# Values of the second layer projected with tokens on the partitions, and the bonus as one column per token

## The chip, the cores and the metric

The kernel runs on one core of one Trainium2 chip. The metric is the device time of one execution in microseconds. Before the change it is 4623.11 us, the median of 3 runs (4621.35 to 4625.97).

## The reference

One inference step of a two-layer streaming encoder. It works on a prompt of 2048 tokens and on 8 running streams of 16 tokens each, with 1024 channels, all in fp32. The first layer is a gated DeltaNet mixer, the second an RWKV-7 time mixer; each adds its output to x, and a last RMS norm follows. The change lies in the second layer alone:

```python
rkvz = jnp.einsum('gbtd,dge->gbte', xs[:4], w_in.reshape(D, 4, W_B)).astype(f32)
r, k, v, z = rkvz[0], rkvz[1], rkvz[2], rkvz[3]
...
k = k * (1.0 + (a - 1.0) * k_a.astype(f32))
...
S, o = lax.scan(step, s0.astype(f32), seq)
...
o = (o - mean) * lax.rsqrt(var + GN_EPS) * gn_w + gn_b
o = o + jnp.sum(r * k * r_k.astype(f32), axis=-1, keepdims=True) * v
o = o.reshape(B, T, W_B) * jax.nn.silu(z)
y = o.astype(h.dtype) @ w_out
```

There are 16 heads of 64 channels. The values v enter twice: in the recurrence over tokens (the scan), and in the bonus, the sum over a head's channels of r, k and r_k, times v. The bonus's sum is one number per token and head.

## The kernel before, in words

Every projection is done with split operands: each fp32 matrix is a high and a low part in fp32r, and three products (high by high, high by low, low by high) make one. On TensorE the stationary operand is the one that is loaded first, the moving one streams past it, and the result has as many rows as the stationary one has columns.

The second layer works on 6 blocks of tokens (`B_BLOCKS`): the first has 2 chunks of 64 prompt tokens and the 128 sample tokens (256 columns), the five others 6 chunks each (384 columns). Its work is of two kinds.

*The stream* (`b_stream`) projects the blocks: for each block the kinds k (1), r (0), the two low-rank hidden layers (4, 5), v (2) and z (3), in units of 128 output channels, two units at a time, each in a PSUM bank of its own (tag "mm", 2 banks). A pair of units is 8 steps; a step takes one weight tile of 128x256 and makes 6 products (lines 1062 to 1064). The weight tile is stationary and the tokens move, so the result has channels on the partitions and tokens in the columns. `b_keep` copies a finished bank on ScalarE (line 1084) and stores it to DRAM (`kvd`). Where v is needed, its tile is loaded again as V (line 1097), again with channels on the partitions. The stream runs about one block ahead of the rest.

*The pair steps* (`b_steps`) work on 48 pairs (8 pairs of heads in 6 blocks). In step i five stages of different pairs run beside each other: `b_prep` of pair i, `b_subst` of i-1, `b_inverse` of i-2, `b_scan` of i-3, `b_gate` of i-4, and `b_out` of two finished pairs at each second step, and 17 steps of the stream (8 in the last 8 pairs). A step has 12 rounds (`rounds`). A stage written as a generator gets its next piece in the round given for it, in the order prep, inverse, gate, subst, scan, out, stream. This order holds on TensorE alone, which is the one engine in `MANUAL`.

On the other engines and on the DMA queue of SyncE a list scheduler orders the instructions by due times. `_due` computes these from the log of all instructions: an instruction's due time is the place of the first TensorE instruction that needs what it writes, less a lead (6 places, 40 for a DMA), through as many instructions as lie between; what nobody needs soon gets a slack of 300 places.

Where the values and the bonus come in before the change:

- `b_prep` forms kp (line 1159) and rk = r times r_k times kp (line 1163) on VectorE. In round 5 TensorE makes the sums of squares of the keys as one column per chunk (line 1188). In round 7 the bonus's sum is one product with a block matrix of 0.5 (line 1198), which gives the sum on every channel row, and VectorE multiplies it with V (line 1200): `bv`.
- `b_inverse` turns V, chunk by chunk and head by head, with the identity (line 106, from `turn`) in its fifth piece, which is round 5, and ScalarE copies the result into `XV` (line 1327), which the scan reads.
- `b_scan` has for each chunk a product with XV (line 1382), a second product (1393) and the state's update by VectorE into the next chunk's part of XV (line 1395) and into R (line 1396).
- `b_centre` and `b_gate` normalise the scan's output OC with tokens on the partitions (line 1476 on GpSimd is the last pass), turn it back in round 6 (line 106), then on VectorE multiply with the norm's weight, add bv (line 1485), add the norm's bias and multiply with the z path (line 1486). The result is split (lines 162 and 163) for `b_out` (lines 168 to 170).

## Time and profile before

| | |
|---|---|
| profiled execution | 4610.68 us |
| its span, first to last instruction | 4608.9 us |
| TensorE busy | 4299.8 us (93%) |
| VectorE busy | 3470.3 us (75%) |
| ScalarE busy | 2287.8 us (50%) |
| GpSimd busy | 1749.9 us (38%) |
| mean granted TensorE clock | 0.966 |

One execution is profiled, and its durations are those of the rows below. PE is TensorE, PEld its weight loads, DVE VectorE, ACT ScalarE, POOL GpSimd, SP SyncE. L1198 is line 1198 of the kernel. An fp32 product shows as two instructions, an fp32r product as one. Products are pipelined: their ends are modelled and overlap, so the distance of two starts tells what one takes of the engine's time.

### The profile page before, as it was taken

What the parts mean: (1) busy time and instruction counts of PE and PEld (TensorE: products, weight loads), DVE (VectorE), ACT (ScalarE), POOL (GpSimd) and SP (SyncE); (2) the same over time, 40 slices, a digit from 0 to 9 for tenths busy, and PEclk for the clock granted to TensorE, in tenths of its full rate; (3) what the DMA queues carried; (4) which work ended last, traced back from release to release, by engine and by line L of the source; (5) the groups of instructions that cost most, each with busy time, mean ns of one, the idle gap of its engine ahead of it and who ended that gap; (6) DMA issues with size and microseconds to landing.
All of it is one profiled execution on the core that took longest, in us unless ns stands there. A gap on an engine that the chain in (4) does not pass through costs nothing. (4 is left out here: it accounts for less than half of the span.)

```text
span 4608.9 us, 104071 instructions
## 1 busy us (share of the span) xinstructions
PE 4299.8 (93%) x37093; PEld 3697.1 (80%) x37093; DVE 3470.3 (75%) x9203; ACT 2287.8 (50%) x6132; POOL 1749.9 (38%) x2507
## 2 busy tenths in 40 slices
PE   7999999999999999999987889999999999999996
PEld 6888788888888899999986767778787887887775
DVE  7888776676666776766677888877778778777885
ACT  5554454454344434444466665655455446446543
POOL 7666543322111211112103555445444434344441
PEclk9999999999999999999998989999999999999997
DMA  6666665556445576666655667766675665665542
GB/s 192 210 202 207 211 208 172 174 187 192 142 140 159 174 212 186 183 213 188 179 159 175 206 196 229 223 179 196 191 203 166 197 206 163 201 195 146 145 129 72
DMA packets 765670, 842.18 MB, mean 183 GB/s; under 512 B 263480, under 2 KB 497360, under 8 KB 765152
## 3 DMA queue, kind: packets, MB, share of 16 engines
q1 hardware_dynamic: 765152, 835.53, 59.9%
q8 instruction: 294, 4.82, 0.4%
q14 instruction: 224, 1.84, 0.1%
HBM read 632.73 MB, written 202.53 MB: 181 GB/s over the span
## 5 line engine op out<-in xcount | busy, mean ns | idle before, releaser
L453 PE MATMUL ps<-hh,whl 128*128 128x384 f32 (+1 forms) x1960 | 795.3, 406 | 12.8 <-ACT hh L162 10.6
L455 PE MATMUL ps<-hh,whl 128*128 128x384 f32 (+1 forms) x1960 | 711.8, 363 | 6.9 <-POOL whl L125 6.7
L454 PE MATMUL ps<-hl,whl 128*128 128x384 f32 (+1 forms) x1960 | 710.9, 363 | 1.7 <-DVE hl L163 1.4
L1062 PE MATMUL ps<-xh,whl 128*128 128x384 f32 (+1 forms) x1632 | 605.3, 371 | 32.0 <-ACT xh L162 17.4
L1063 PE MATMUL ps<-xl,whl 128*128 128x384 f32 (+1 forms) x1632 | 557.8, 342 | 22.0 <-POOL xl L163 11.2
L1064 PE MATMUL ps<-xh,whl 128*128 128x384 f32 (+1 forms) x1632 | 556.8, 341 | 9.2 <-DVE whl L125 8.8
L125 POOL TENSOR_TENSOR whl<-wraw,whl 128x256 fp32r<-128x256 f32 x454 | 374.6, 830 | 358.6 <-ACT whl L124 331.5
L573 DVE SCALAR_TENSOR_TENSOR cv<-pre,cw,cv 128x512 f32<-128x512 f32 (+3 forms) x576 | 375.3, 660 | 134.9 <-ACT cv L571 130.2
L453 PEld LDWEIGHTS ps<-hh,whl 128*128 128x128 f32 x1960 | 371.9, 190 | 65.8 <-issue 14.1
L168 PE MATMUL ps<-oh,whl 128*128 128x384 f32 (+2 forms) x1024 | 390.3, 381 | 26.6 <-DMA whl<-wd 13.9
L124 ACT CAST whl<-wraw 128x256 fp32r<-128x256 f32 x726 | 287.2, 402 | 255.5 <-DMA wraw<-in_w_b 74.3
L455 PEld LDWEIGHTS ps<-hh,whl 128*128 128x128 f32 x1960 | 371.4, 189 | 48.2 <-POOL whl L125 12.7
L454 PEld LDWEIGHTS ps<-hl,whl 128*128 128x128 f32 x1960 | 372.7, 190 | 34.0 <-DVE hl L163 4.6
L1062 PEld LDWEIGHTS ps<-xh,whl 128*128 128x128 f32 x1632 | 320.7, 197 | 75.3 <-ACT xh L162 23.0
L169 PE MATMUL ps<-ol,whl 128*128 128x384 f32 (+2 forms) x1024 | 366.8, 358 | 7.6 <-DVE ol L163 7.6
L844 DVE TENSOR_TENSOR sbt<-B,TB 48x15 f32<-48x15 f32 (+14 forms) x1320 | 351.9, 267 | 22.3 <-DMA B<-scr 1.7
L170 PE MATMUL ps<-oh,whl 128*128 128x384 f32 (+2 forms) x1024 | 363.6, 355 | 1.8 <-POOL whl L125 1.8
L846 DVE TENSOR_TENSOR TB<-TB,sbt 48x15 f32<-48x15 f32 (+14 forms) x1320 | 348.9, 264 | 19.8
L1063 PEld LDWEIGHTS ps<-xl,whl 128*128 128x128 f32 x1632 | 322.5, 198 | 33.8 <-POOL xl L163 17.2
L1064 PEld LDWEIGHTS ps<-xh,whl 128*128 128x128 f32 x1632 | 321.7, 197 | 16.8 <-DVE whl L125 16.2
L822 DVE TENSOR_TENSOR x<-x,ps 128x384 f32<-128x384 f32 (+1 forms) x320 | 191.1, 597 | 79.4 <-PE ps L170 77.9
L168 PEld LDWEIGHTS ps<-oh,whl 128*128 128x128 f32 x1024 | 196.6, 192 | 66.1 <-ACT oh L162 10.7
(349 smaller groups left out, 10233.7 us busy)
## 6 DMA issues: line engine op xcount, KB each, us to landing
whl<-wd SPq DMA_DIRECT2D x1582, 256.0 KB
wd<-whl SPq DMA_DIRECT2D x428, 256.0 KB
wraw<-in_w_a SPq DMA_DIRECT2D x288, 128.0 KB
wraw<-in_w_b SPq DMA_DIRECT2D x256, 128.0 KB
kvd<-kvo SPq DMA_DIRECT2D x160, 192.0 KB
xn<-x1d SPq DMA_DIRECT2D x80, 192.0 KB
wraw<-in_w_ao SPq DMA_DIRECT2D x96, 128.0 KB
xn<-in_x SPq DMA_DIRECT2D x32, 256.0 KB
```

What stands on the lines that cost most here:

```text
L125: (self.nc.gpsimd if tag == "o" else self.weng).tensor_tensor(w[:, 1], raw, w[:, 0].bitcast(F32), op=SUB)
L168: self.nc.tensor.matmul(out, lhsT=wh, rhs=hh, start=first and i == 0, stop=False)
L169: self.nc.tensor.matmul(out, lhsT=wh, rhs=hl, start=False, stop=False)
L170: self.nc.tensor.matmul(out, lhsT=wl, rhs=hh, start=False, stop=i == n - 1)
L453: nc.tensor.matmul(p, lhsT=wh[:, k % 2], rhs=hh, start=k == 0, stop=False)
L454: nc.tensor.matmul(p, lhsT=wh[:, k % 2], rhs=hl, start=False, stop=False)
L455: nc.tensor.matmul(p, lhsT=wl[:, k % 2], rhs=hh, start=False, stop=k == KT - 1)
L573: nc.vector.scalar_tensor_tensor(o, f(j), self.cw[:, ct, j:j + 1], o, op0=MUL, op1=ADD)
L844: nc.vector.tensor_tensor(o, B[:, j + 1:16, j:j + 1].to_broadcast([rows, m, j + 1]), T[:, j:j + 1, 0:j + 1].to_broadcast([rows, m, j + 1]) ...
L1062: nc.tensor.matmul(o, lhsT=wh[:, i], rhs=xh, start=k == 0, stop=False)
L1063: nc.tensor.matmul(o, lhsT=wh[:, i], rhs=xl, start=False, stop=False)
L1064: nc.tensor.matmul(o, lhsT=wl[:, i], rhs=xh, start=False, stop=k == KT - 1)
```

## The change

In the stream the values' units are computed the other way round: the token tile `xh[:, ts]` of 128 tokens is stationary, and 256 columns of the weights move, two units at once. The weight tile of a step now holds one of the 8 input tiles for 256 output channels (two pieces of 512 bytes a row in the first load). The result has tokens on the partitions. Of the 384 tokens two tiles of 128 share the first bank and the third lies in the second; since three sums begin in two banks, a product of a zero tile with 512 columns clears the first bank. `b_keep_values` copies each token tile on ScalarE and stores it to `vt` in DRAM, tokens as rows. V is no longer loaded and not turned: `b_inverse` loads each head's values from `vt` straight into XV.

The bonus's sum becomes one column per chunk in `b_prep`, as the keys' sums are, right behind them in round 5; ScalarE halves it (`bs`). The bonus times the values is formed by GpSimd in `b_inverse` with tokens on the partitions, and is added in `b_gate` before the turn back. So the norm's weight is multiplied there too, by a table `gw` whose rows repeat over the tokens; behind the turn one VectorE pass is left.

```diff
-NCI, NXH, NOH, NKO = 2, 8, 2, 2
+NCI, NXH, NOH, NKO = 2, 8, 2, 3
...
+                    if g == 2:
+                        self.b_values(b, 2 * s + j, wh, wl, p)
+                        if s == 3 and j:
+                            self.b_keep_values(b, first[1], p)
...
+    def b_values(self, b, k, wh, wl, p):
+
+        xh, xl = b["X", 2, k]
+        wh, wl = [w.rearrange("p j c -> p (j c)") for w in (wh, wl)]
+        if k == 0:
+            self.nc.tensor.matmul(p[0], lhsT=self.zero.to_broadcast([P, P]), rhs=wh.unsqueeze(1).to_broadcast([P, 2, 256]), start=True, stop=False)
+        for t in range(b["NT"] // P):
+            o, ts = p[t // 2][:, t % 2 * 256:t % 2 * 256 + 256], slice(t * P, (t + 1) * P)
+            self.nc.tensor.matmul(o, lhsT=xh[:, ts], rhs=wh, start=k == 0 and t == 2, stop=False)
+            self.nc.tensor.matmul(o, lhsT=xl[:, ts], rhs=wh, start=False, stop=False)
+            self.nc.tensor.matmul(o, lhsT=xh[:, ts], rhs=wl, start=False, stop=k == KT - 1 and t > 0)
+
+    def b_keep_values(self, b, q, p):
+        for t in range(b["NT"] // P):
+            v = self.sp.tile([P, 256], F32, name=self.nm("kvo"), tag="kvo", bufs=NKO)
+            self.nc.scalar.copy(v, p[t // 2][:, t % 2 * 256:t % 2 * 256 + 256])
+            self.nc.sync.dma_start(b["vt"][t * P:(t + 1) * P, q * P:q * P + 256], v)
...
-        for g, n, bufs in ((1, "K", 2), (0, "R", 1), (2, "V", 3)):
+        for g, n, bufs in ((1, "K", 2), (0, "R", 1)):
...
+        pb = self.ps("g")
+        for c in range(nq):
+            for h, hs in enumerate(HS):
+                nc.tensor.matmul(pb[HS[1 - h], c:c + 1], lhsT=c3(rk)[hs, c], rhs=self.ones[hs, 0:1], start=True, stop=True,
+                                 tile_position=(64 * h, 64 - 64 * h))
...
-        pbn = self.ps("g")
-        nc.tensor.matmul(pbn[:, 0:NT], lhsT=cb[:, B_BO:B_BO + P], rhs=rk, start=True, stop=True)
-        bv = self.lp.tile([P, NT], F32, name=self.nm("bv"), tag="bv", bufs=4)
-        nc.vector.tensor_tensor(bv, pbn[:, 0:NT], V, op=MUL)
+        bs = self.mp.tile([P, 8], F32, name=self.nm("bs"), tag="bs", bufs=3)
+        nc.scalar.activation(bs[:, 0:nq], pb[:, 0:nq], AF.Copy, scale=0.5)
...
+        for h in range(2):
+            os, vs = HS[1 - h], slice(q * P + 64 * h, q * P + 64 * h + 64)
+            nc.sync.dma_start(XV[os, 0:nq, h], vt[:, :, vs])
...
-        pt = self.ps("g")
-        for c in range(nq):
-            for h, hs in enumerate(HS):
-                self.turn(pt[HS[1 - h], c * 64:(c + 1) * 64], c3(V)[hs, c], h, 1 - h)
...
-            nc.scalar.copy(XV[os, 0:nq, h], c3(pt[os, 0:nq * 64]))
+            nc.gpsimd.tensor_tensor(bv[os], XV[os, 0:nq, h], d["bs"][os, 0:nq].unsqueeze(2).to_broadcast([64, nq, 64]), op=MUL)
...
+        nc.vector.tensor_tensor(OC, OC, self.gw[:, q:q + 1].to_broadcast([P, nq, 64]), op=MUL)
+        nc.vector.tensor_tensor(OC, OC, d["bv"], op=ADD)
...
-        og = d["bv"]
-        nc.vector.scalar_tensor_tensor(og, pu[:, 0:NT], self.hp[:, q, 3:4], og, op0=MUL, op1=ADD)
-        nc.vector.scalar_tensor_tensor(og, og, self.hp[:, q, 4:5], SZ, op0=ADD, op1=MUL)
+        og = d["bv"].rearrange("p c v -> p (c v)")
+        nc.vector.scalar_tensor_tensor(og, pu[:, 0:NT], self.hp[:, q, 4:5], SZ, op0=ADD, op1=MUL)
```

## Rows read from the trace of the kernel before

**Rows 1.** Windows, one pair step: us, engines' busy us (count), clock, DMA share, GB/s.

```profile
3363.60:3415.50 51.90, 48.06 (x531) 41.82 (x530) 37.47 (x93) 20.68 (x58) 22.97 (x27) 0.93 0.71 205
```

**Rows 2.** Waits of TensorE, 2800 to 4400 us: us in total, times, longest.

```profile
PE ps L1382 <- DVE XV L1395: 37.5, 28, 2.6
```

**Rows 3.** Groups of instructions by shape: count | busy us, mean ns | idle before.

```profile
L106 PE MATMUL ps<-ident,V 64*64 64x64 f32 x1088 | 43.0, 225 | 0.0
...
L1188 PE MATMUL ps<-ones,ch 64*64 64x1 f32 x1088 | 40.3, 196 | 4.1 <-POOL ch L1161 4.1
...
L1198 PE MATMUL ps<-ch,cb 128*128 128x384 f32 x80 | 33.8, 504 | 2.3 <-DVE ch L1163 1.9 <-DVE TB L846 0.4
```

**Rows 4.** Timeline of TensorE, behind the bonus: start us, us, instruction, idle before it.

```profile
2911.03 0.81 PE L1198 MATMUL ps<-ch,cb 128*128 128x384 f32 x2
2911.77 0.34 PE L1382 MATMUL ps<-XV,GM 128*64 128x64 f32 x4
...
3373.57 0.80 PE L1382 MATMUL ps<-XV,GM 128*64 128x64 f32 x4 [2.25 <-DVE XV L1395]
```

**Rows 5.** Timeline of VectorE, the scan's state at the same two places.

```profile
2909.99 0.59 DVE L1395 SCALAR_TENSOR_TENSOR XV<-ps,wc,Sw 64x64 f32<-64x64 f32 x2
...
3372.72 0.60 DVE L1485 SCALAR_TENSOR_TENSOR bv<-ps,hp,bv 128x384 f32<-128x384 f32 x1
3373.25 0.59 DVE L1395 SCALAR_TENSOR_TENSOR XV<-ps,wc,Sw 64x64 f32<-64x64 f32 x2
3373.88 0.62 DVE L1486 SCALAR_TENSOR_TENSOR bv<-bv,hp,SZ 128x384 f32<-128x384 f32 x1
```

**Rows 6.** Timeline of TensorE, products of 256 and of 384 columns.

```profile
2508.38 0.28 PE L1064 MATMUL ps<-xh,whl 128*128 128x256 f32 x1
...
2508.73 0.28 PE L1064 MATMUL ps<-xh,whl 128*128 128x256 f32 x1
...
3302.17 0.34 PE L169 MATMUL ps<-ol,whl 128*128 128x384 f32 x1
...
3303.05 0.34 PE L1062 MATMUL ps<-xh,whl 128*128 128x384 f32 x1
```

**Rows 7.** Timelines of TensorE and ScalarE, between two pairs of the values' units.

```profile
2468.24 0.38 PE L1062 MATMUL ps<-xh,whl 128*128 128x256 f32 x1
...
2467.82 0.37 ACT L1084 COPY kvo<-ps 128x256 f32<-128x256 f32 x1
...
3131.62 0.44 PE L1062 MATMUL ps<-xh,whl 128*128 128x384 f32 x1
...
3131.23 0.48 ACT L1084 COPY kvo<-ps 128x384 f32<-128x384 f32 x1
```

**Rows 8.** Timelines of VectorE and TensorE: kp, rk and the keys' column products.

```profile
3451.47 0.54 DVE L1159 TENSOR_TENSOR ch<-ch,K 128x384 f32<-128x384 f32 x1
...
3459.12 0.60 DVE L1163 SCALAR_TENSOR_TENSOR ch<-R,prm,ch 128x384 f32<-128x384 f32 x1
...
3453.16 0.69 PE L1188 MATMUL ps<-ones,ch 64*64 64x1 f32 x18
```

**Rows 9.** Timelines of GpSimd and TensorE: the gate's last pass and its turn.

```profile
3363.44 0.83 POOL L1476 TENSOR_TENSOR OC<-OC,gn 128x384 f32<-128x384 f32 x1
...
3368.03 0.92 PE L106 MATMUL ps<-ident,OC 64*64 64x64 f32 x24
```

**Rows 10.** Lines 1225 and 1236 (ns min/median/max), then timelines of GpSimd and VectorE.

```profile
L1225 POOL TENSOR_TENSOR N<-GM,m x36: 827/1020/1137, 2837.8 to 4395.4; 64x384 f32<-64x384 f32 x36
...
L1236 SPq DMA_DIRECT2D scrb<-N x72: 577/581/1375, 2843.5 to 4397.4; - x72
...
3462.10 4.48 POOL L1181 TENSOR_TENSOR BK<-ch,ch 64x384 f32<-64x384 f32 x4 [0.51 <-ACT ch L1152]
...
3462.23 1.03 DVE L846 TENSOR_TENSOR TB<-TB,sbt 48x39 f32<-48x39 f32 x1
...
3366.81 0.18 DVE L846 TENSOR_TENSOR TB<-TB,sbt 48x39 f32<-48x39 f32 x1
```

More of the change, by code (lines that the diff above doesn't have):

```diff
@@ L908, in b_setup_side @@
         nc.vector.tensor_scalar(mu[:, 1], mu[:, 0], -1.0, 1.0, op0=MUL, op1=ADD)
+        self.zero = bp.tile([P, 1], F32R, name="zero")
+        nc.gpsimd.memset(self.zero.bitcast(F32), 0.0)
         hc = bp.tile([P, KT, 1], F32, name="hc")
@@ L922, in b_setup @@
         nc.vector.tensor_scalar(hp[:, :, 5:6], hp[:, :, 2:3], -1.0, 1.0, op0=MUL, op1=ADD)
+        gw = bp.tile([P, KT, 64], F32, name="gw")
+        for h in range(2):
+            nc.sync.dma_start(gw[64 - 64 * h:P - 64 * h].rearrange("p q v -> p (q v)"), io["b_gw"][h, :].partition_broadcast(64))
+        nc.vector.tensor_scalar(gw, gw, 0.5, None, op0=MUL)
+        self.gw = gw
         sm = bp.tile([P, NB], F32, name="smb")
@@ L1039, in srcs @@
                     for j in range(2):
-                        yield ("b", g, q, s, j), w[:, s, 2 * j:2 * j + 2], b["off"]
+                        yield ("b", g, q, s, j), w[:, s, j:4:2] if g == 2 else w[:, s, 2 * j:2 * j + 2], b["off"]
         yield from self.b_hidden(blocks[0])
@@ L1057, in b_stream @@
                     wh, wl = next(W)
+                    if g == 2:
+                        self.b_values(b, 2 * s + j, wh, wl, p)
+                        if s == 3 and j:
+                            self.b_keep_values(b, first[1], p)
                     o = p[j][:, 0:NT]
-                    for i in range(2):
+                    for i in range(2 if g != 2 else 0):
                         k = 2 * s + i
@@ L1064, in b_stream @@
                         nc.tensor.matmul(o, lhsT=wl[:, i], rhs=xh, start=False, stop=k == KT - 1)
-                    if s == 3:
+                    if s == 3 and g != 2:
                         self.b_keep(b, g, q, p[j])
@@ L1271, in b_inverse @@
         T, Tt = Ts
+        ex = 2 * b["nsc"]
+        TM = self.lp.tile([P, nq + ex, 2, 64], F32, name=self.nm("TM"), tag="TM", bufs=2)
+        XV = self.lp.tile([P, nq + ex, 2, 64], F32, name=self.nm("XV"), tag="XV", bufs=2)
+        VS = self.lp.tile([P, 2 * ex, 64], F32, name=self.nm("VS"), tag="VS", bufs=2) if ex else None
+        assert (2, q) in b["kept"]
+        vt = b["vt"].rearrange("(c t) x -> t c x", t=64)
+        for h in range(2):
+            os, vs = HS[1 - h], slice(q * P + 64 * h, q * P + 64 * h + 64)
+            nc.sync.dma_start(XV[os, 0:nq, h], vt[:, :, vs])
+            if ex:
+                nc.sync.dma_start(VS[os, 0:ex], vt[:, ncp:nq, vs])
         N16 = self.lp.tile([P, ncp, 64], F32, name=self.nm("N16"), tag="ci", bufs=NCI)
@@ L1318, in b_inverse @@
         yield
-        pt = self.ps("g")
-        for c in range(nq):
-            for h, hs in enumerate(HS):
-                self.turn(pt[HS[1 - h], c * 64:(c + 1) * 64], c3(V)[hs, c], h, 1 - h)
-        if ex:
-            nc.scalar.copy(VS[:, 0:ex], c3(pt[:, ncp * 64:nq * 64]))
+        bv = self.lp.tile([P, nq, 64], F32, name=self.nm("bv"), tag="bv", bufs=3)
         for h in range(2):
             os = HS[1 - h]
-            nc.scalar.copy(XV[os, 0:nq, h], c3(pt[os, 0:nq * 64]))
+            nc.gpsimd.tensor_tensor(bv[os], XV[os, 0:nq, h], d["bs"][os, 0:nq].unsqueeze(2).to_broadcast([64, nq, 64]), op=MUL)
+        d["bv"] = bv
         yield
```

14 lines of the change are left out of this document (7 added, 7 removed).

## The prediction

> **What bounds the kernel now.** I read the page's busy times first, then the windows of single pair steps, then the waits of TensorE, and then the timelines of TensorE and VectorE where the diff cuts. The second layer runs from about 2450 us to the end, 48 pair steps of 25 to 57 us. In an ordinary step TensorE is busy 48.06 of 51.90 us, VectorE 37.47, ScalarE 20.68, GpSimd 22.97, and the granted clock there is 0.93 [rows 1]. So TensorE's work sets the pace, and what it doesn't work is short waits. The largest of these is for one thing: in the 1600 us from 2800 to 4400 the scan product on line 1382 waited 37.5 us, 28 times, for the state that VectorE writes on line 1395 [rows 2]. A microsecond taken off TensorE's queue is therefore a microsecond won only where no such wait stands right behind it. Where one does, VectorE's order decides. I price each part with this test.
>
> **The change part by part.**
>
> *The bonus product goes.* Line 1198 is one fp32 product of 384 columns per pair, shown as two instructions, 504 ns each [rows 3]. From its start to the next start on TensorE it holds the queue 0.74 us (2911.03 to 2911.77) [rows 4]. What comes right behind it is, from the twelfth pair on, the scan product of line 1382, and I went through all 48 places in the timeline. In 14 of them the state had been written long before, as here, where VectorE was done at 2910.58 [rows 5], 1.19 us before the scan product: these win all of 0.74, together 10.4 us. In 12 TensorE stands idle behind the bonus until line 1395 is done, as at 3373.57 after 2.25 us [rows 4]: these win nothing. In 11 the state came within that 0.74 us: they win 3.0 us together. In the first 11 pairs a projection or output product follows, and the starts are 0.24 to 0.6 us apart: 3.7 us. Sum: 17.1 us off the path, of some 33 us of queue. Bounds: 0 and 33.
>
> *The turn of the values goes, the bonus column comes.* In round 5 of a step stand today 24 instructions that turn the values (line 106) behind 24 one-column products (line 1188). After the change 24 more one-column products stand in the place of the turn. 1088 turns took 43.0 us and 1088 one-column products 40.3 us [rows 3]: I take nothing, bound 2.7 us of gain. ScalarE loses two copies of the turned values and gains one tiny scaling. It is off the path, and I take nothing for that.
>
> *The bonus column needs its input two rounds earlier.* The products of round 5 now read rk (line 1163), which the old bonus product read in round 7. In 30 of the 48 pairs rk was finished only after round 5's products had started. The typical case: products at 3453.16, rk done at 3459.72, while kp, its input on line 1159, was done at 3452.01 [rows 8]. Taken over all pairs the lateness adds up to 113 us. But rk was not late for lack of input: it lay ready some 7 us and VectorE did other things, because the planner's due time came from round 7. With the new due time it can run right behind kp, and be done 0.6 us after it [rows 8], before the product. Kp itself ended after the products in nine pairs, all among the first twelve and the last three, by some 31 us in all when rk's 0.6 is counted behind it; kp's due time moves with rk's, and I leave an eighth: +4 us. Bounds: 0 and +113. Behind the waiting column stand, in TensorE's one queue, the scan step of that round and a projection.
>
> *The values' projection.* Six old products of 384 columns per chunk become nine of 256. Starts are 0.176 us apart at 384 columns (five steps from 3302.17 to 3303.05) and 0.117 us at 256 (three steps from 2508.38 to 2508.73) [rows 6], and there too each product has its own weight load. 72 times 0.117 is 8.4 us, 48 times 0.176 is 8.4 us: nothing. The clearing product of 512 columns is new, 24 times; by twice the 256 pitch it is 0.235 us: +5.7 us.
>
> *Both banks come full together.* Before, the bank of the first unit was copied out while the second was still being filled. Now the next pair of units waits for two ScalarE copies of 256 columns, 0.37 us each [rows 7]. In the later blocks the next projection starts at 3131.62 where ScalarE began its copy at 3131.23: two copies end at 3131.97, 0.35 us late. Such a busy ScalarE stands at some 8 of the 20 boundaries: 2.8 us. In the first block the next product follows at 2468.24 and two copies from 2467.82 end at 2468.56 [rows 7], and at another of the four ScalarE came a microsecond later: 0.7 us each, 2.8 us. Together +5.6 us, bounds 0 and 18 (24 times 0.74).
>
> *The gate.* VectorE gains two passes over OC ahead of the turn back and loses the product on line 1200 and one of the two passes behind the turn, lines 1485 and 1486: an equal number. Ahead of the turn there is room: OC was ready at 3364.27 and turned at 3368.03 [rows 9], one of the closest of the ordinary steps; most have 7 to 18 us. Only the last pair of all has none: two passes more before and one less behind is one pass of 0.6 us at the end of the kernel, +0.6. The pass that goes behind the turn matters more. In nearly all pairs from the ninth on, line 1485 stands right ahead of line 1395 in VectorE's order: 3372.72, then the state at 3373.25, then line 1486 at 3373.88 [rows 5]. If the one remaining pass takes line 1486's place, the state is 0.53 us earlier: 12 idle places give 6.4 us and the 11 half-covered ones 4.5 us more. If it takes line 1485's place, nothing comes. I take -8. Bounds: -11 and 0.
>
> *GpSimd and the loads.* The bonus times the values is two products of 64x384 with a broadcast on GpSimd; the nearest row is line 1225, 1.02 us [rows 10]. Two microseconds of an engine that idles half of each step [rows 1], needed only two steps later: hidden, but they may push another GpSimd product: +2, bounds 0 and 26 (below). The load of V (one issue) becomes two loads into XV of 64 rows and 256-byte pieces, issued in round 1 of the third step and used from round 5. The nearest row on SyncE's queue is the store of N, 0.58 us an issue [rows 10]: 1.2 us a step against one issue less, and half an issue more for the values' stores. Behind them stand the weight loads, which are issued ahead. I take nothing; a cover lost here would show as waits for whl.
>
> **Sum.** -17.1 +0 +4 +0 +5.7 +5.6 +0.6 -8 +2 = -7.2 us. The profiled execution took 4610.68 us (span 4608.9), so 4603.5; the median of the timed runs, 4623.11, stands 0.27% above it, and on that scale the forecast is 4616 us. About 0.2% (9 us) is what a measurement can tell from no change, so the forecast lies just inside.
>
> **Rivals.**
>
> *Slower: the bonus column waits for rk.* If VectorE keeps rk where it is, round 5 stalls in 30 pairs, in all 113 us [rows 8], and idle of 2 us was followed by stretches at half clock in step 3363 to 3415 (0.93 on the mean) [rows 1, 4]. All of it: 4603.5 - 4 + 113, scaled 4725. A third of it: +38, 4654. It decides the sign from 16 us on, a seventh. For it: 30 of 48 pairs; against it: the input was there, and the due time moves. Chance 0.17, mostly a third to a half.
>
> *Faster: the queue's whole saving comes through.* If shorter VectorE work before line 1395 also closes the 12 idle places, the bonus wins 33, the state 11, and no new wait appears: -33 -11 +5.7 = -38, scaled 4585. For it: VectorE is busy under three quarters of a step [rows 1]. Against it: the idle places came about by VectorE's order, not its load. Chance 0.22.
>
> *GpSimd holds up VectorE.* While the four 64x384 products of line 1181 ran for 4.48 us, a small VectorE product took 1.03 us, where the same shape took 0.18 at another place [rows 10]. 96 new products that each hold a VectorE instruction 0.8 us are 77 us, and a third of that on TensorE's path is +26: 4603.5 - 2 + 26, scaled 4640. Against it: the new products have a broadcast operand like line 1225. Chance 0.06. The Trainium skill, "SBUF — State Buffer", section "SBUF: two separate sides", says that GpSimd and those VectorE instructions that read two SBUF operands take one port pair by turns, for a whole instruction. By that rule this rival would apply to the new products too; the rows agree for line 1181.
>
> *The bonus was hidden anyway.* If the scan's waits take up what goes, the 17.1 is nothing and the sum is +10: 4633. Chance 0.10.
>
> **How the numbers follow.** Forecast 0.45, its own range 4604 to 4630, because evacuation, rk and the gate pass can each be off by a few us; of it 0.19 is faster, 0.225 within 0.2%, 0.035 slower. The faster rival gives 0.21 faster and 0.01 the same; rk 0.16 slower and 0.01 the same; GpSimd 0.05 and 0.01; the hidden bonus 0.055 slower and 0.045 the same. Together faster 0.40, same 0.30, slower 0.30. The range runs from the faster rival's time, 4585, to 4662, which holds rk's third and leaves its worse half out.
>
> **What would show it.** Right: line 1188's group doubles and its wait for line 1163 is under 10 us; the wait of the scan product for line 1395 falls in spite of the bonus gone; the new last pass of the gate stands behind line 1395 on VectorE; the wait of the first projection product for the values' copies stays under 10 us. Wrong: TensorE waiting for rk in many pairs, VectorE instructions of a microsecond beside the new GpSimd products, or waits for whl.

## The result and the profile after

The changed kernel takes 4750.41 us (median; 4738.3 to 4765.91), the kernel before beside it 4624.54. The ratio is 1.0272, 95% interval 1.0247 to 1.0296: 126 us slower, outside the range given. The execution profiled here took 4765.91 us, the longest of the four; the one profiled before took 4610.68 us, shorter than all of the timed ones. So the two profiles lie 155 us apart where the medians lie 126 apart. In this document a ratio is turned into us by 4624.5.

First the page of the kernel after (busy time and share of the span by engine), then the second layer as one window of each kernel: us, busy us (count) of PE, PEld, DVE, ACT, POOL, granted clock, DMA share, GB/s.

```profile
span 4764.2 us, 104941 instructions
PE 4375.8 (92%) x37501; PEld 3795.4 (80%) x37501; DVE 3525.8 (74%) x9204; ACT 2257.1 (47%) x6096; POOL 1804.2 (38%) x2604
```

```profile
2450.00:4608.90 2158.90, 1954.66 (x22661) 1644.78 (x22660) 1703.78 (x4625) 1132.86 (x3120) 975.93 (x1238) 0.94 0.60 180
```

```profile
2450.00:4764.20 2314.20, 2020.18 (x23085) 1731.70 (x23084) 1764.88 (x4649) 1108.05 (x3101) 1035.37 (x1354) 0.89 0.58 169
```

The loss lies in the second layer: its span grows from 2158.90 to 2314.20, by 155 us, in the two profiled executions. TensorE's idle time (span less busy) grows from 204 to 294 us, its busy time by 66. But the clock fell from 0.94 to 0.89. Summed over the clock records of the traces, the lower level of 1.2 GHz held for 251 us before and 515 after, with TensorE busy for 210 and 418 us of it. Half of that taken off, the work at full clock is 1850 us before and 1811 after. This is an estimate: products of 384 columns start 0.320 us apart at the lower level and 0.175 us at the upper one, a little under twice, and with that ratio the two are 1860 and 1831. So the change did take some 30 to 40 us of work off TensorE's queue, and idle time (+90) and lower clock (+95 to +104) took back about five times that. Some 30 of these 155 us lie between executions and not between kernels: the granted clock of the whole run was 0.937 in this execution and 0.942 in the three others.

Where the idle time is, in the waits of the kernel after: TensorE from 2800 to 4400 us (this answers [rows 2]), then from 2450 on TensorE's and VectorE's (us in total, times, longest).

```profile
PE ps L1420 <- DVE XV L1433: 45.3, 35, 3.6
```

```profile
PE ps L1225 <- DVE ch L1194: 26.8, 14, 5.0
PE ps L168 <- DMA whl<-wd: 19.5, 21, 2.1
PE ps L1090 <- ACT kvo L1100: 12.0, 3, 4.2
DVE OC L1515 <- POOL OC L1514: 99.4, 47, 5.6
```

No wait of TensorE is large enough for 90 us, and the scan product's wait has grown where the prediction had it fall (37.5 to 45.3 us). Added up by the engine waited for, TensorE's waits from 2450 us on went from 101 to 166 us for VectorE, from 34 to 58 for ScalarE, from 43 to 41 for GpSimd and from 15 to 19 for DMAs. So most of the new idle time is in many small waits for VectorE. The large new row stands on VectorE: the first new pass of the gate (line 1515, times the norm's weight) waits in 47 of the 48 pairs for GpSimd's product over OC (line 1514, the old line 1476 of [rows 9]), 2.1 us each. What that does is seen in one place. The timeline of the kernel after, GpSimd, VectorE, ScalarE, TensorE (start, us, instruction, idle before it and its releaser):

```profile
3176.61 0.82 POOL L1303 TENSOR_TENSOR T<-cm,cb 128x384 f32<-128x384 f32 x1
3177.40 0.72 POOL L125 TENSOR_TENSOR whl<-wraw,whl 128x256 fp32r<-128x256 f32 x1
3178.09 0.82 POOL L1303 TENSOR_TENSOR T<-cm,cb 128x384 f32<-128x384 f32 x1
3178.87 1.31 POOL L110 TENSOR_TENSOR gn<-gn,half 128x6 f32<-128x6 f32 x1
3180.26 0.83 POOL L1514 TENSOR_TENSOR OC<-OC,gn 128x384 f32<-128x384 f32 x1
3181.05 0.99 POOL L1320 TENSOR_TENSOR N<-N,cb 128x384 f32<-128x384 f32 x1
...
3175.73 0.17 DVE L1512 TENSOR_SCALAR gn<-gn 128x6 f32<-128x6 f32 x1
3181.12 1.33 DVE L1515 TENSOR_TENSOR OC<-OC,gw 128x384 f32<-128x384 f32 x1 [5.22 <-POOL OC L1514]
3182.49 0.56 DVE L1516 TENSOR_TENSOR OC<-OC,bv 128x384 f32<-128x384 f32 x1
3182.97 0.95 DVE L1170 TENSOR_TENSOR_SCAN ch<-smb,ch 128x384 f32<-128x384 f32 x1
...
3183.95 0.52 ACT L1178 ACTIVATE Ep<-ch 128x384 f32<-128x384 f32 x1 [4.69 <-DVE ch L1170]
3184.50 0.92 ACT L1100 COPY kvo<-ps 128x256 f32<-128x256 f32 x3
...
3185.20 0.80 PE L1090 MATMUL ps<-whl,zero 128*128 128x512 f32 x1 [3.76 <-ACT kvo L1100]
```

VectorE gives the statistics (3175.73), but GpSimd has the three products shown, and copies before them, ahead of its power (line 110) and its product. VectorE stands for 5.22 us. Behind its two passes is the decay's scan (line 1170), for which ScalarE stands 4.69 us; behind that on ScalarE are the copies that empty the values' banks, and for these TensorE stands 3.76 us. The profile puts TensorE's wait down to ScalarE, three engines from where it began.

The answers to [rows 1, 3, 6]: the same pair step (from the 22nd pair's key columns to the 23rd's), the two groups of one-column products, and two rows of the new projection, 0.82 us and seven starts apart.

```profile
3427.80:3482.40 54.60, 47.52 (x529) 42.13 (x528) 36.99 (x102) 20.48 (x57) 23.36 (x30) 0.94 0.64 191
```

```profile
L1225 PE MATMUL ps<-ones,ch 64*64 64x1 f32 x1088 | 44.0, 203 | 27.8 <-DVE ch L1194 26.8 <-DVE m L1229 1.0
L1219 PE MATMUL ps<-ones,ch 64*64 64x1 f32 x1088 | 42.6, 201 | 12.8 <-POOL ch L1192 12.8
```

```profile
4363.12 0.27 PE L1094 MATMUL ps<-whl,xl 128*128 128x256 f32 x1
...
4363.94 0.28 PE L1095 MATMUL ps<-whl,xh 128*128 128x256 f32 x1
```

The products cost what was forecast (0.117 us a start, 44.0 us for 1088 columns). What was not forecast is the waiting: the step took 54.60 in place of 51.90 us with TensorE no busier in it.

Of the prediction's four signs of being right, half of one came true: a second group of 1088 one-column products stands beside line 1188's (line 1219 now). But its wait for rk is 26.8 us and not under 10, the scan's wait rose, the clearing product waits 12.0 us for the values' copies (line 1090) and not under 10, and the gate's remaining pass (line 1525) does not stand behind the state's instruction (line 1433). It stands right ahead of it in 35 of the 40 pairs from the ninth on, as line 1485 did before. VectorE after:

```profile
3492.16 0.62 DVE L1525 SCALAR_TENSOR_TENSOR bv<-ps,hp,SZ 128x384 f32<-128x384 f32 x1 [1.41 <-PE ps L106]
3492.69 0.59 DVE L1433 SCALAR_TENSOR_TENSOR XV<-ps,wc,Sw 64x64 f32<-64x64 f32 x2
```

### The profile page after: what moved, and what is told of

It reads as the page before. It is cut to its first block, busy times and chain, and to the rows that moved or that the text cites. A ratio compares the mean times of both kernels' runs of the same rounds, so it can differ in the third digit from the quotient of the medians.

```text
span 4764.2 us, 104941 instructions
## 1 busy us (share of the span) xinstructions
PE 4375.8 (92%) x37501; PEld 3795.4 (80%) x37501; DVE 3525.8 (74%) x9204; ACT 2257.1 (47%) x6096; POOL 1804.2 (38%) x2604
## 5 line engine op out<-in xcount | busy, mean ns | idle before, releaser
L1074 PE MATMUL ps<-xh,whl 128*128 128x384 f32 (+1 forms) x1248 | 477.0, 382 | 27.8 <-ACT xh L162 12.2
L1076 PE MATMUL ps<-xh,whl 128*128 128x384 f32 (+1 forms) x1248 | 441.7, 354 | 15.9 <-DVE whl L125 15.6
L1075 PE MATMUL ps<-xl,whl 128*128 128x384 f32 (+1 forms) x1248 | 440.2, 353 | 12.5 <-DVE xl L163 7.8
L1074 PEld LDWEIGHTS ps<-xh,whl 128*128 128x128 f32 x1248 | 255.1, 204 | 62.4 <-ACT xh L162 16.5
L1076 PEld LDWEIGHTS ps<-xh,whl 128*128 128x128 f32 x1248 | 256.7, 206 | 24.4 <-DVE whl L125 23.8
L1075 PEld LDWEIGHTS ps<-xl,whl 128*128 128x128 f32 x1248 | 257.5, 206 | 20.0 <-DVE xl L163 12.2
```

The lines of the kernel that those rows point to most:

```text
L1074: nc.tensor.matmul(o, lhsT=wh[:, i], rhs=xh, start=k == 0, stop=False)
L1075: nc.tensor.matmul(o, lhsT=wh[:, i], rhs=xl, start=False, stop=False)
L1076: nc.tensor.matmul(o, lhsT=wl[:, i], rhs=xh, start=False, stop=k == KT - 1)
```

## The experiments

"The changed kernel" is the version after; each ratio is to the kernel before on the same chip.

### First: the columns, the clock, the projection

In the second layer of the changed kernel's trace 25 of the 67 drops of the clock began within 4 us of the end of the bonus's columns, and TensorE waited 26.8 us for rk there.

**e1_wide**: 64 columns in place of one.

```diff
-                nc.tensor.matmul(pb[HS[1 - h], c:c + 1], lhsT=c3(rk)[hs, c], rhs=self.ones[hs, 0:1], start=True, stop=True,
+                nc.tensor.matmul(pb[HS[1 - h], c * 64:(c + 1) * 64], lhsT=c3(rk)[hs, c], rhs=self.ones[hs, 0:64], start=True, stop=True,
...
-        nc.scalar.activation(bs[:, 0:nq], pb[:, 0:nq], AF.Copy, scale=0.5)
+        nc.scalar.activation(bs[:, 0:nq], pb[:, 0:64 * nq:64], AF.Copy, scale=0.5)
```

> The changed kernel, but the 24 bonus products of round 5 have 64 columns each (64 times the same sum; one of them is read), as the turn of the values had in their place. Order and waits are unchanged. Theory clock (the one-column products, together with the idle time behind them, let TensorE's clock fall to 1.2 GHz): the granted clock returns from 0.94 to about 0.96 and the time from 4750 to 4640-4680, ratio to before about 1.005 to 1.012. Rival wait (the loss is rk's lateness and VectorE's order): nothing moves, 4740-4760, ratio 1.027, clock 0.94.

Measured: 4752.85 us, 1.0265 (1.0241 to 1.0289), mean granted clock 0.945 after 0.937 in the profiled executions (0.947 after 0.941 over the four of each). The clock rose and the time did not follow: TensorE idles 313 us of the second layer in place of 294.

**e2_late**: the same columns two rounds later, where the bonus stood before.

```diff
+        m2 = self.mp.tile([P, 2, 8], F32, name=self.nm("m2"), tag="m2", bufs=4)
...
+        yield
+        yield
+
         pb = self.ps("g")
...
-        m2 = self.mp.tile([P, 2, 8], F32, name=self.nm("m2"), tag="m2", bufs=4)
...
         d["bs"] = bs
-        yield
-        yield
         yield
         yield
```

> The changed kernel, but the bonus products (one column each) stand in round 7, where the old bonus product stood, so rk is needed as late as before. Theory wait: the 26.8 us of waits for rk go and most of the loss with them, 4640-4680. Theory clock: the 27 us go, and the stretch of one-column products in round 5 is halved, so that part of the clock comes back too: 4680-4715, clock 0.945-0.955.

Measured: 4768.74 us, 1.0312 (1.0285 to 1.034). Both theories had expected a gain. The wait for rk is all but gone from the trace (0.9 us), but the scan's wait for its state (from 2450 us on) is 68.3 us in place of 55.9, and TensorE's idle time there only falls from 294 to 284. Most of the rk wait stood in front of waits that come anyway.

**e3_late_wide**: both edits.

> The changed kernel with both: bonus products of 64 columns in round 7. Round 5 has then 24 one-column products and neither turn nor bonus. Theory clock: round 5 is still poor in columns before its idle time, so no better than the wide one in round 5 except for rk's 27 us: 4630-4670. Theory wait: as the late one, within 5 us of it.

Measured: 4753.12 us, 1.0269 (1.0252 to 1.0286). So neither the place nor the shape of the columns is the cause; what the columns themselves cost is a question for e11 and e15 below.

**e4_old_projection**: the values projected the old way, with XV's loads as they are.

```diff
-                    for i in range(2 if g != 2 else 0):
+                    for i in range(2):
...
-        vt = b["vt"].rearrange("(c t) x -> t c x", t=64)
+        vt = b["kv"][2, q].rearrange("p t -> (p t)").rearrange("(c t x) -> t c x", t=64, x=P)
```

> The changed kernel, but the values are projected in the old way (weights stationary, 384 columns, two banks that fill one after the other, no clearing product); the loads into XV read the stored tile as if it were rows of tokens, so the values are wrong and only the time counts. If the projection and its copies cost what the prediction said, the time falls by about 11 us, to 4740. If the new projection is what lets the clock fall (its products of 256 columns, the stall between the units): 4650-4700.

Measured: 4758.4 us, 1.0292 (1.0269 to 1.0316). No gain in either of the expected ranges: the new projection costs nothing that can be told here.

### Second: the gate

**e5_no_passes**: without the two passes.

```diff
         nc.gpsimd.tensor_tensor(OC, OC, g[:, 0, 0:nq].unsqueeze(2).to_broadcast([P, nq, 64]), op=MUL)
-        nc.vector.tensor_tensor(OC, OC, self.gw[:, q:q + 1].to_broadcast([P, nq, 64]), op=MUL)
-        nc.vector.tensor_tensor(OC, OC, d["bv"], op=ADD)
```

> The changed kernel without VectorE's two new passes over OC ahead of the turn (lines 1515 and 1516), so the norm's weight and the bonus are left out of the output; all else stands. Theory gate (VectorE, which takes its instructions in order, stands idle 99 us in front of GpSimd's product on line 1514, and the two passes take 0.99 and 0.75 us instead of 0.55): 4620-4660, ratio 0.999 to 1.007, VectorE's wait for line 1514 gone. Rival loads (the bonus products on GpSimd, the 256-byte loads into XV): 4715-4745; only the passes' own 84 us of VectorE go, of which TensorE sees a part.

Measured: 4693.16 us, 1.0135 (1.011 to 1.016). Half of the loss is in these two lines, and half is not, which the theory did not expect.

**e6_before_two_passes**: the kernel before with two passes at that place.

```diff
         nc.gpsimd.tensor_tensor(OC, OC, g[:, 0, 0:nq].unsqueeze(2).to_broadcast([P, nq, 64]), op=MUL)
+        for _ in range(2):
+            nc.vector.tensor_tensor(OC, OC, self.ones[:, 0:64].unsqueeze(1).to_broadcast([P, nq, 64]), op=MUL)
```

> The kernel before, plus two passes on VectorE over OC behind GpSimd's product and ahead of the turn (times 1.0, so nothing changes in the output). Theory gate: the wait comes into the kernel before and costs nearly what the change cost, 4710-4760; the two passes here come without the two that the change removed, so it may be a little more. Rival loads: the passes fit into VectorE's idle quarter, 4625-4660.

Measured: 4704.21 us, 1.0163 (1.0147 to 1.0179), 75 us, a little under the gate theory's range. It takes nothing else of the change.

**e7_passes_gpsimd**: both passes on GpSimd (`nc.vector` to `nc.gpsimd` in the two lines).

> The changed kernel with both passes over OC on GpSimd instead of VectorE: nothing on VectorE waits for line 1514 any more, GpSimd has some 2 us more per pair. Theory gate: 4630-4670. Rival loads, or GpSimd as the holder of VectorE: no better than the change, 4740-4780.

Measured: 4728.99 us, 1.0219 (1.0202 to 1.0236), between the two expected ranges. VectorE's wait is gone, but against e5, which has no passes at all, the two on GpSimd cost 39 us (± 14), and VectorE is 36 us busier than there (3501.9 after 3466.0) with the same 9108 instructions. GpSimd's work is not free either.

**e8_weight_first**: the weight ahead of GpSimd's product, the bonus added by GpSimd.

```diff
+        nc.vector.tensor_tensor(OC, OC, self.gw[:, q:q + 1].to_broadcast([P, nq, 64]), op=MUL)
         self.pow(g[:, 0, 0:nq], g[:, 1, 0:nq], -1)
         nc.gpsimd.tensor_tensor(OC, OC, g[:, 0, 0:nq].unsqueeze(2).to_broadcast([P, nq, 64]), op=MUL)
-        nc.vector.tensor_tensor(OC, OC, self.gw[:, q:q + 1].to_broadcast([P, nq, 64]), op=MUL)
-        nc.vector.tensor_tensor(OC, OC, d["bv"], op=ADD)
+        nc.gpsimd.tensor_tensor(OC, OC, d["bv"], op=ADD)
```

> The changed kernel, but the norm's weight is multiplied by VectorE ahead of GpSimd's two passes (in its place behind the variance), and the bonus is added by GpSimd: VectorE keeps one pass and waits for nothing new. Theory gate: 4625-4665, a few us better than both passes on GpSimd. Rival loads: 4720-4750.

Measured: 4695.76 us, 1.0146 (1.012 to 1.0173), above the theory's range, but within the error of the version without the passes (e5), with all of the work done.

**e9_next_round**: the two passes one round later.

```diff
         nc.gpsimd.tensor_tensor(OC, OC, g[:, 0, 0:nq].unsqueeze(2).to_broadcast([P, nq, 64]), op=MUL)
+        yield
         nc.vector.tensor_tensor(OC, OC, self.gw[:, q:q + 1].to_broadcast([P, nq, 64]), op=MUL)
         nc.vector.tensor_tensor(OC, OC, d["bv"], op=ADD)
         yield
-        yield
```

> The changed kernel with the two new VectorE passes over OC (times the norm's weight, plus the bonus) one scheduling round later: behind the first of the three rounds that stand between GpSimd's product over OC and the turn back, in place of directly behind that product. No instruction is added or left out. Theory gate: the loss sits in the wait of the pass times the weight for GpSimd's product (99 us in 47 waits in the changed kernel's trace) and in what is queued behind it on VectorE; a round later GpSimd is mostly done, so that wait falls below 30 us and the time to 4690 to 4710 us, near the version without the passes (4693). Rival busy: two passes of 0.99 and 0.75 us cost by their own time (83 us of VectorE) wherever they stand; then it stays at 4735 to 4755. Rival late: a round later the sum comes too late for the turn back, and TensorE waits there for OC instead (6 us in one wait in the changed kernel); then that group grows to over 30 us and the time stays above 4730.

Measured: 4756.05 us, 1.0265 (1.0242 to 1.0288), within 1 us of what "busy" expected. But it told nothing: the wait is the same to the last digit, for a round in the text orders TensorE alone, and VectorE goes by due times, which the edit hardly moved (its order differs in 35 of 9204 places). The waits of this version's VectorE:

```profile
DVE OC L1516 <- POOL OC L1514: 99.4, 47, 5.6
```

**e13_passes_ahead**: the two passes of e6 in the kernel before, ahead of GpSimd's product.

```diff
+        for _ in range(2):
+            nc.vector.tensor_tensor(OC, OC, self.ones[:, 0:64].unsqueeze(1).to_broadcast([P, nq, 64]), op=MUL)
         self.pow(g[:, 0, 0:nq], g[:, 1, 0:nq], -1)
         nc.gpsimd.tensor_tensor(OC, OC, g[:, 0, 0:nq].unsqueeze(2).to_broadcast([P, nq, 64]), op=MUL)
```

> The kernel before with two VectorE passes over OC (times 1.0) ahead of GpSimd's product over OC in the gate, in place of behind it; the version with the same two passes behind it took 1.0163 times the kernel before. Theory place: what costs is that VectorE, in order, stands behind a GpSimd product; ahead of it nothing new is waited for, so the same two passes cost at most 20 us: 4630 to 4650. Rival busy: some 80 us more of VectorE's time cost as much as behind GpSimd, 4690 to 4710 us. Between them (4650 to 4690) both have a share.

Measured: 4645.66 us, 1.0032 (1.0018 to 1.0046). The same instructions in the same kernel cost 15 us ahead of GpSimd's product and 75 behind it: the place, and not the work to be done. The passes' groups from 2450 us on (count, busy us, mean ns, idle before), of e6 and of e13:

```profile
L1478 DVE TENSOR_TENSOR OC<-OC,ones 128x384 f32<-128x384 f32 x80 | 72.1, 901 | 83.8 <-POOL OC L1476 83.3
```

```profile
L1476 DVE TENSOR_TENSOR OC<-OC,ones 128x384 f32<-128x384 f32 x80 | 53.2, 665 | 0.0
```

83.3 us of standing in 40 pairs against none, and passes that last 901 ns behind GpSimd's product and 665 ahead of it.

### Third: the other half

**e12_old_values**: the values all on their old way (projection, load of V, turn, copies), neither the passes nor GpSimd's bonus products. Against the kernel before: the columns come, the bonus product and two VectorE passes go. (The edit is shown against the kernel before.)

```diff
-        nc.tensor.matmul(pbn[:, 0:NT], lhsT=cb[:, B_BO:B_BO + P], rhs=rk, start=True, stop=True)
-        nc.vector.tensor_tensor(bv, pbn[:, 0:NT], V, op=MUL)
+                nc.tensor.matmul(pb[HS[1 - h], c:c + 1], lhsT=c3(rk)[hs, c], rhs=self.ones[hs, 0:1], start=True, stop=True,
+        nc.scalar.activation(bs[:, 0:nq], pb[:, 0:nq], AF.Copy, scale=0.5)
...
-        nc.vector.scalar_tensor_tensor(og, pu[:, 0:NT], self.hp[:, q, 3:4], og, op0=MUL, op1=ADD)
-        nc.vector.scalar_tensor_tensor(og, og, self.hp[:, q, 4:5], SZ, op0=ADD, op1=MUL)
+        nc.vector.scalar_tensor_tensor(og, pu[:, 0:NT], self.hp[:, q, 4:5], SZ, op0=ADD, op1=MUL)
```

> The version without the two passes and without GpSimd's bonus products, and with the values on their old way: the other form of projection, one load of V per pair, its turn by TensorE and two copies by ScalarE into XV. Against the kernel before it has the bonus columns in place of the bonus product of 384 columns, one VectorE pass over the bonus and one of the gate less, and an unused ScalarE copy per pair (the bonus and the norm's weight are left out of the output). Theory GpSimd: the columns and the values' way matter little, so it ends near the version without GpSimd's products, at 4610 to 4660 us, and no more than 20 us from it. Rival loads: the values' new way is what costs, so it falls to 4600 to 4620 while the version with the new way stays at 4680 to 4695. Rival columns: it stays at 4660 to 4690 like the version with the new way.

Measured: 4633.17 us, 1.0005 (0.9988 to 1.0022): as the kernel before, within the error.

**e18_old_projection_loads**: the same with XV's loads in place of V's load, turn and copies (the edit against e12).

```diff
-                self.turn(pt[HS[1 - h], c * 64:(c + 1) * 64], c3(V)[hs, c], h, 1 - h)
-            nc.scalar.copy(XV[os, 0:nq, h], c3(pt[os, 0:nq * 64]))
+            nc.sync.dma_start(XV[os, 0:nq, h], vt[:, :, vs])
```

> The version without the two passes and without GpSimd's bonus products (1.0053 times the kernel before), with the values projected the old way and stored as channels; the loads into XV stay, 64 rows in 256-byte pieces, and read those values in the wrong order (values, norm's weight and bonus are wrong in the output, the work is the same). With turn and copies in place of the loads as well it was 1.0005. Theory loads: the loads, with no turn, are what costs the half per cent; then 4645 to 4655 us (1.0035 to 1.006). Rival projection: the 256-column products, the clearing product and the two full banks cost it; then 4625 to 4638 us (0.999 to 1.002).

Measured: 4652.18 us, 1.0057 (1.0039 to 1.0076), 24 us (± 12) more than e12. The windows from 2450 us to the end, e12 and then e18:

```profile
2450.00:4624.60 2174.60, 1963.62 (x23656) 1676.90 (x23656) 1676.51 (x4547) 1143.35 (x3178) 977.72 (x1257) 0.93 0.61 180
```

```profile
2450.00:4654.60 2204.60, 1963.56 (x22604) 1667.94 (x22604) 1680.23 (x4566) 1108.20 (x3095) 956.51 (x1258) 0.91 0.62 178
```

**e10_no_bonus_product**: with the new projection as well, that is the changed kernel without the passes and without GpSimd's bonus products (the edit against e5).

```diff
-            nc.gpsimd.tensor_tensor(bv[os], XV[os, 0:nq, h], d["bs"][os, 0:nq].unsqueeze(2).to_broadcast([64, nq, 64]), op=MUL)
```

> The version without the two passes (4693 us) and also without GpSimd's two bonus products per pair (96 of 0.96 us); it leaves out the norm's weight and the bonus. Theory GpSimd: these 92 us on GpSimd make what follows on that engine late and lengthen VectorE's passes beside them; without them 4645 to 4665 us, and VectorE's passes over rk and the input splits go back from 0.91 and 0.63 to about 0.70 and 0.58 us. Rival loads: what is left of the loss comes from XV's loads in 256-byte pieces and the values' way through memory; then 4680 to 4695. Rival columns: it comes from the one-column products of the bonus and the earlier wait for rk; then also 4680 to 4695.

Measured: 4648.86 us, 1.0053 (1.0034 to 1.0071). So the loads in place of the turn cost 0.5%, the projection nothing, and GpSimd's products 0.8% (1.0053 to 1.0135). The DMA totals from 2450 us on, of e12 and of e18:

```profile
DMA packets 396873, 390.73 MB, mean 180 GB/s; under 512 B 172752, under 2 KB 288927, under 8 KB 396575
```

```profile
DMA packets 429803, 392.54 MB, mean 178 GB/s; under 512 B 210786, under 2 KB 321613, under 8 KB 429514
```

Nearly the same bytes in 33,000 more packets. That this is how the loads cost is not shown: TensorE's waits for DMAs did not grow (17.2 us in e12, 16.9 in e18). What grew are its waits for VectorE (97 to 123 us) and ScalarE (31 to 42).

**e19_old_values_gpsimd**: GpSimd's products put back into e12, behind ScalarE's copies, their result unused (the line that e10 takes out).

> The version with the values on their old way, without the two passes and without GpSimd's bonus products (1.0005 times the kernel before), with those two GpSimd products per pair put back, reading XV behind ScalarE's copies; their result is not used (norm's weight and bonus are left out of the output). Theory GpSimd: the products cost by themselves, as they did beside the new loads (1.0053 to 1.0135); then 4655 to 4675 us (1.006 to 1.010). Rival together: they cost only where the values' new way has used up the slack; then 4628 to 4645 (0.9995 to 1.003).

Measured: 4695.64 us, 1.0145 (1.0123 to 1.0168): 65 us in a kernel that has nothing else of theirs. Busy time in the whole execution, e12 and then e19, and a wait of e19's GpSimd:

```profile
PE 4317.0 (93%) x38085; PEld 3736.2 (81%) x38085; DVE 3439.3 (74%) x9107; ACT 2296.0 (50%) x6180; POOL 1749.2 (38%) x2508
```

```profile
PE 4350.2 (93%) x38085; PEld 3770.5 (80%) x38085; DVE 3490.9 (74%) x9107; ACT 2294.4 (49%) x6180; POOL 1835.0 (39%) x2604
```

```profile
POOL bv L1357 <- ACT XV L1353: 79.4, 29, 9.0
```

GpSimd is 86 us busier, as it should be. VectorE is 52 us busier with the same 9107 instructions: they last longer beside GpSimd's. In this version GpSimd also stands 79 us for ScalarE's copies, which the changed kernel (loads) does not. That may be why the products cost 65 us here (above both expected ranges) and 38 there; it is not shown.

**e17_scalar_bonus**, with **e16_first_late_wide** beside it: e8's and e3's edits together (e16), and then the bonus products on ScalarE (the edit against e16).

```diff
-            nc.gpsimd.tensor_tensor(bv[os], XV[os, 0:nq, h], d["bs"][os, 0:nq].unsqueeze(2).to_broadcast([64, nq, 64]), op=MUL)
+            for c in range(nq):
+                nc.scalar.activation(bv[os, c], XV[os, c, h], AF.Copy, scale=d["bs"][os, c:c + 1])
```

> The changed kernel with two mends together: the weight multiplied by VectorE ahead of GpSimd's product and the bonus added by GpSimd (that alone took 1.0146 times the kernel before), and the bonus's products in round 7 with 64 columns each (that alone changed nothing beside the passes' wait). Theory columns: with the passes' wait gone the earlier need for rk and the dropped clock decide, so the move now gives 25 to 45 us: 4650 to 4670. Rival: what the version without columns won was the products themselves and not their place or shape; then 4680 to 4700.

> The same two mends, and the values times the bonus made by ScalarE, 12 products of 64 x 64 per pair, in place of GpSimd's two of 64 x 384. Theory GpSimd: GpSimd's 92 us of these products cost 38 us by making its later work and VectorE's passes late; ScalarE is busy under half of the span, so most of that comes back: 20 to 35 us below the version with the two mends alone. Rival load: any engine of the chain that is loaded so pays for it; 12 small products of about 0.2 us (some 115 us in all) make ScalarE's copies late for the scan, and the time is the same as that version or up to 30 us above it.

Measured: 4702.52 us, 1.016 (1.0138 to 1.0183), and 4676.56 us, 1.0101 (1.0075 to 1.0127). Moving the columns gives nothing without the passes' wait either. Twelve small products on ScalarE are 0.6% cheaper than two on GpSimd (27 us ± 16), though ScalarE is then 144 us busier than in e16 (2401.0 after 2256.7). This is the fastest version that does all of the changed kernel's work, and it is slower than the kernel before.

**e11_no_columns**: e5 without the bonus's columns (the bonus's scale is read from the keys' columns).

```diff
-                nc.tensor.matmul(pb[HS[1 - h], c:c + 1], lhsT=c3(rk)[hs, c], rhs=self.ones[hs, 0:1], start=True, stop=True,
...
-        nc.scalar.activation(bs[:, 0:nq], pb[:, 0:nq], AF.Copy, scale=0.5)
+        nc.scalar.activation(bs[:, 0:nq], pn[:, 0:nq], AF.Copy, scale=0.5)
```

> The version without the two passes (4693 us) and also without the 24 one-column products of the bonus per pair; ScalarE's copy reads the columns of the squared norms in their place, so GpSimd's products run as before on other numbers (the bonus and the norm's weight are left out of the output). TensorE no longer waits for rk in that round. Theory columns: the products with one column and the wait for rk (11 us in that version) are what drops the clock and leaves the rest of the loss; then 4645 to 4665 us with a mean granted clock above 0.955. Rivals GpSimd and loads: only the products' own queue time and the rk wait go, some 10 to 15 us: 4675 to 4685.

Measured: 4648.52 us, 1.0045 (1.0028 to 1.0061), 42 us (± 14) less than e5. The time is the columns theory's, the clock is not: it is 0.949 in the profiled execution, after 0.947 in e5.

**e15_columns_beside**: the columns and their copy added to the kernel before.

> The kernel before with the changed kernel's 24 one-column products of the bonus per pair and ScalarE's small copy of them added in round 5; its own bonus product of 384 columns stays in round 7, so nothing is left out. Theory columns: the earlier need for rk and the products' own time cost 25 to 45 us by themselves, as taking them from the version without the passes gave 45: 4650 to 4670 us, with TensorE's wait for rk at those products 8 to 15 us in the trace. Rival together: they cost only where GpSimd's bonus products also delay kp and rk; then 4630 to 4645 and a wait for rk below 8 us.

Measured: 4645.32 us, 1.0038 (1.0021 to 1.0056), 18 us. TensorE's wait for rk at the columns is 13.0 us in its trace, and TensorE is busy 1989.19 us of the second layer after 1954.66, 34.5 us more: the columns cost mainly their own time. That taking them from e5 won 42 us (± 14) and adding them here lost 18 (± 8) is not settled further.

## Why the prediction was wrong

Going down the steps, each difference with the error that its two intervals give when taken as independent:

| step | forecast us | measured us | from |
|---|---|---|---|
| bonus product -17.1, rk +4, gate pass behind the turn -8; columns with the turn still there (+18 by e15) | -3 | +2 ± 8 | before to e12 |
| turn gone (it was to give back the columns' 18), loads 0 | -18 | +24 ± 12 | e12 to e18 |
| projection, clearing product, full banks | +11 | -2 ± 12 | e18 to e10 |
| GpSimd's bonus products | +2 | +38 ± 14 | e10 to e5 |
| two passes ahead of the turn back | +0.6 | +63 ± 16 | e5 to after |

The 18 us of e15 are no part of the forecast: the first row has the columns and the turn together, which the forecast never had, and the second row gives them back.

**The step that failed is the gate's.** It counted the passes: "an equal number. Ahead of the turn there is room". The room is there (3.76 us from GpSimd's end to the turn in [rows 9]) and TensorE hardly waits for OC after the change either. But the prediction asked who waits for the passes, and not for what they wait and what stands behind them. The passes it took away hardly waited in the kernel before (line 1485 13.1 us in all, for the turn; lines 1200 and 1486 not at all); the new ones wait 99.4 us for GpSimd, which runs late and in its own order. e6 and e13 show it without the rest of the change: 75 us behind GpSimd's product, 15 ahead of it. In the changed kernel the two passes cost 63 us (± 16) where the forecast had +0.6. The prediction's own test, whether a wait stands right behind, was put to TensorE's queue alone; put to VectorE's it would have pointed there.

The other half of that step was -8 us for the pass behind the turn. Its own condition names the case that came: the remaining pass took line 1485's place ahead of the state, for which the prediction had "nothing".

**GpSimd's products** were taken as hidden for the reason that GpSimd idles half of each step. The step's range (0 to 26) ended below the measured 38, if within its error of 14. The rival that named the mechanism, VectorE held up, had the chance of 0.06 and the price +26. VectorE 52 us busier in e19 and 36 us in e7, without a new instruction, bears the mechanism out, and the reason against it ("a broadcast operand like line 1225") did not hold. How much of the cost comes this way, and how much from GpSimd's later work being late, no run separates.

**Turn and loads.** The prediction set the columns against the turn and the loads at nothing, and looked for a lost cover in waits for whl. The swap is right by its counts (44.0 us of columns after, 43.0 of turns before). But with the turn gone and the loads in its place TensorE's busy time did not fall (1963.6 us in e12 and in e18 both), its idle time rose from 211 to 241 us and the granted clock fell from 0.961 to 0.951. By the estimate used above, the work at full clock did fall, by 29 us, and the lower clock took all of it back. So it is open whether the loads bring the loss or the missing turn does: waits for whl did not grow, and no kernel was run that has the loads in larger pieces or both the loads and the turn.

**Right within their bounds**: the projection (e4, e10), the bonus product and rk. The bonus product was not taken out alone; e12 and e15 differ by it and two VectorE passes, and e12 is 15 us (± 11) faster, where the forecast has -17.1 and -8. So the agreement of the table's first row (-3 and +2) is in part luck, for the -8 is in it. The wait for rk came, 26.8 us where 4 was taken and 113 was the end of the bounds, but e2 and e3, which remove it, are no faster: other waits take its place. (One slip hangs on nothing: a third of the rk wait, priced as the whole is, gives 4650 and not 4654.) The main rival of the slower side was the right sign by the wrong wait.

The sum of the table's measured column is 125 us, but only because it follows one path; taken in another order the steps share differently (the columns: 18 us in the kernel before, 42 in e5).

## What to carry to other kernels

An instruction that is moved behind another engine's work is priced by three questions: what it waits for, how late that engine runs, and what is queued behind it on its own engine; its duration and its number are the smallest part. Put the pass ahead of the slow engine's instruction where the arithmetic allows (a weight times a scale commutes), as e8 did. And where TensorE's work sets the pace but four engines hand work round, an engine that is busy 40% of the time is not free: the loss appears as small waits for other engines, with the clock falling beside them (e13 to e6: idle 225 to 264 us of the second layer, lower level 259 to 316).

## What the runs showed of the hardware

- The granted clock cost about as much as the idle time that came with it. Of the 155 us between the two profiles 90 are idle and an estimated 95 to 104 lower clock, less the work saved. Raising the clock by wider products (e1: 0.937 to 0.945) did not shorten the run.
- VectorE and GpSimd lengthen each other. In the timeline above line 1515 began 0.07 us after GpSimd's line 1320 and took 1.33 us. At 4366.06 it began 0.05 us ahead of GpSimd's bonus product and took 0.56 us, and then GpSimd's took 1.20 in place of 0.85 us. The timelines of GpSimd and VectorE after:

```profile
4366.11 1.20 POOL L1364 TENSOR_TENSOR bv<-XV,bs 64x384 f32<-64x384 f32 x1
...
3185.20 0.85 POOL L1364 TENSOR_TENSOR bv<-XV,bs 64x384 f32<-64x384 f32 x1
...
4366.06 0.56 DVE L1515 TENSOR_TENSOR OC<-OC,gw 128x384 f32<-128x384 f32 x1 [3.83 <-POOL OC L1514]
```

  The Trainium skill, "SBUF — State Buffer", section "SBUF: two separate sides", says that of a GpSimd instruction and a VectorE instruction that reads two SBUF operands, whichever starts first has the shared port pair for its whole instruction while the other waits. Both places agree in their order, and here each instruction has a broadcast operand.
- In the timeline above VectorE, ScalarE and GpSimd each go on in the order in which they were given their work, and a standing instruction holds all behind it: from one late product VectorE stands 5.22 us, ScalarE 4.69 and then TensorE 3.76. The Trainium skill, "PSUM — Partial Sum Buffer", section "Engine vs sequencer instructions", says the same of these three queues ("strict FIFO"), and the trace agrees.
